# Encoder trunk: TensorE in written order, state-space work in pairs of steps, state-space input matrices made without TensorE

## The chip, the cores and the metric

One core of one Trainium2 chip runs the whole program. The metric is device time in microseconds (us) from start to end of one execution. Of the kernel before there are three runs and one profiled execution.

## The reference, cut to what matters

256 tokens of width 1024 pass through two layers, all in float32. Each layer normalises the tokens, makes one wide input projection, and feeds three branches: retention (four heads), latent attention (eight heads) and a state-space branch (S5). The branches are projected, gated and summed, projected again, and a SwiGLU feed-forward network (FFN) follows. The change lies around the S5 branch:

```python
abar_re = mag * jnp.cos(dt * a_im); abar_im = mag * jnp.sin(dt * a_im)     # 64 groups x 64 states
bb_re = coef_re[..., None] * b_re - coef_im[..., None] * b_im              # group, state, 16 channels
bu_re = jnp.einsum('bsgc,gpc->bsgp', u_g, bb_re)                           # input to the states
_, _, xr, xi = lax.associative_scan(combine, (a_re_t, a_im_t, bu_re, bu_im), reverse=reverse, axis=1)
y = jnp.einsum('bsgp,gcp->bsgc', xr, c_re) - jnp.einsum('bsgp,gcp->bsgc', xi, c_im)
```

The kernels cut the 256 tokens into 32 pieces of 8. Within a piece, the contribution of 8 tokens times 16 channels to a state is one 128 x 128 matrix per group: the input matrix, a product of powers of `abar` (8 of them) and `bb`. There are two directions and 64 groups, so a layer has 16 steps of four groups each; a step's input matrices are 128 x 1024 numbers (512 KB).

## The kernel before, in words

**Main line.** Each weight block of 512 KB (`raw`, five buffers) is fetched by SyncE (SP), which issues every DMA of the kernel. ScalarE (ACT) casts it to a high part `wh` (L668), VectorE (DVE) makes the low part `wl` (L669), and TensorE (PE) makes 24 matmuls, three per product (L673 to L675). The stages of a layer follow one another: the S5 input `u`, retention's projections and heads, the attention's projections and heads, the GLU of S5, the three branch projections, `w_out`, the FFN's gate and up, and its down projection.

**Background.** The S5 work is a Python generator, `s5` (L400). After each weight block, `tick` gives it some credit and it emits some more instructions between those of the main line. All engines are then put in an order by the framework's scheduler, TensorE too, so that what is written in one row may be taken apart.

**Input matrices.** `s5_wt` (L512) makes one step's: four DVE operations from the tables PW (powers) and BB, which lie transposed in SBUF, eight turns of 128 x 128 on PE (L536), and two ACT copies out of PSUM (L538). In layer 0 a step's matrices go at once into the products `pl` (L452: four matmuls of 32 columns by 256). In layer 1 all sixteen are made ahead, mostly under the FFN of layer 0, written to DRAM (`wtd`) and fetched again for `pl`. After two steps, `lq` is copied, turned (L462) and copied into the states SS (L467, L468).

**Output.** `s5_out` (L541) makes per step the output matrices Y (L569 to L573) and the products `pk` (L584: eight matmuls). Per pair of steps `pk` goes through DRAM (`kd`) to be skewed into M (`wt<-kd`, four loads), and `s5_emit` (L615) adds three products per step (L629: 24 matmuls per pair). The four `wt<-kd` loads take their source with an outer dimension of 8.

**Tables.** `s5_params` and `s5_tables` load a, dt and B, with B in runs of 64 bytes (`load_b`), and permute the tables with matmuls against `perm`.

Of the kernel before, what the change touches and what calls it, by code (L numbers as in the profile page):

```python
# [17 lines left out]
P = 128  # L18
# [25 lines left out]
def consts():  # L44
    c = {}
    c["ident"] = np.eye(P, dtype=np.float32)
    perm = np.zeros((P, P), np.float32)
    for d in range(2):
        for qh in range(2):
            for q in range(8):  # L50
                for g4 in range(4):
                    perm[d * 64 + (qh * 4 + g4) * 8 + q, d * 64 + (qh * 8 + q) * 4 + g4] = 1.0
    c["perm"] = perm
# [25 lines left out]
class Kern:  # L79
    def __init__(self, ctx, tc, aps, n4=17, n16=2, nraw=5, nw=3, nwl=3, nwy=3, nwt=2, ntm=2, nev=4, nat=2, r0=75, r1=75, r2=20, delay=1, late=0, e0=2, e1=0, force=0, q0=55, q1=60, nat_u=1, gauss=1, unn=1, ya=0, sp=1, yw=40, yy=30, split=2, m0=4, m1=4, fin=1, dfr=1, nu0=3, nu1=1, pin=0, nl=-1, fw=0, fy=1, ng0=0, ng1=2, tt=1, tp=0, nq0=0, nq1=0, sk=1):  # L80
# [115 lines left out]
    def exp_acc(self, out, z, n):  # L196
        nc, V = self.nc, self.nc.vector
        zc, kf, r, p = (self.s(n, f"xp{n}", 4) for _ in range(4))
        i = self.s(n, f"xi{n}", dt=I32)
# [9 lines left out]
        V.scalar_tensor_tensor(out, p, 1.0, i.bitcast(F32), ALU.add, ALU.mult)  # L209

    def s5_params(self, l):
# [19 lines left out]
        self.exp_acc(mag, z, N)  # L231
# [27 lines left out]
        cf = self.s(2 * SP_, "t_cfn").rearrange("p (r q) -> p r q", r=2)  # L259
        den, t1, t2, nr = (nt(k) for k in ("den", "t1", "t2", "nr"))  # L260
# [22 lines left out]
    def load(self):  # L283
        if self.loads:
            f = self.loads.pop(0)
            if f:
                f()

    def s5_tables(self, l):


        nc, V, A = self.nc, self.nc.vector, self.nc.scalar
        pn, cf = yield from self.s5_params(l)
        yield 4.0
        PX = self.s4().rearrange("p (j d g) -> p j d g", j=8, d=2)
        for b in range(2):
            ps = self.bank(self.p5)
            for j in range(4):
                nc.tensor.matmul(ps[:, j * P:(j + 1) * P], pn[:, b * 4 + j].rearrange("p r q -> p (r q)"),
                                 self.perm, start=True, stop=True)  # L300
            A.copy(PX[:, b * 4:b * 4 + 4].rearrange("p j d g -> p (j d g)"), ps)
        CF = self.s(2 * 64, "t_cf").rearrange("p (r g) -> p r g", r=2)
        ps = self.bank(self.p5)
        nc.tensor.matmul(ps[:, 0:P], cf.rearrange("p r q -> p (r q)"), self.perm, start=True, stop=True)
        for r in range(2):
            for d in range(2):
                A.copy(CF[d * 64:d * 64 + 64, r, :], ps[r * 64:r * 64 + 64, d * 64:d * 64 + 64])
        PW = self.s4().rearrange("p (r s g) -> p r s g", r=2, s=8)
        A8 = self.s(2 * 64, "t_a8").rearrange("p (r g) -> p r g", r=2)
        A8s = self.s(2 * 64, "t_a8s").rearrange("p (r g) -> p r g", r=2)  # L310
        for r in range(2):
            nc.gpsimd.memset(PW[0:64, r, 0, :], 1.0 - r)
            nc.gpsimd.memset(PW[64:128, r, 7, :], 1.0 - r)
            rows = slice(r * 64, r * 64 + 64)
            A.copy(PW[0:64, r, 1:8, :], PX[rows, 0:7, 0, :])
            A.copy(PW[64:128, r, 6::-1, :], PX[rows, 0:7, 1, :])
        for d in range(2):
            rows = slice(d * 64, d * 64 + 64)
            A.copy(A8[rows, 0, :], PX[0:64, 7, d, :])
            A.copy(A8[rows, 1, :], PX[0:64, 7, d, :])  # L320
            A.mul(A8s[rows, 0, :], PX[64:128, 7, d, :], -1.0)
            A.copy(A8s[rows, 1, :], PX[64:128, 7, d, :])
        PXD = self.t(self.dr, [P, 1024], "pxd", 2)
        self.dma(PXD, PX.rearrange("p j d g -> p (j d g)"))
        if l == 0 and self.nl >= 0:
            while "b" not in self.cx:
                yield None
            br, bi = self.cx.pop("b")
        else:
            br, bi = self.s4(), self.s4()  # L330
            for f in self.load_b(l, br, bi):
                f()
        BB = [self.s4(), self.s4()]
        for qh in range(2):
            c = slice(qh * 512, qh * 512 + 512)
            nat = lambda t: t[:, c].rearrange("p (h q c) -> p h q c", h=4, q=8)
            natt = lambda t: t.rearrange("p (h q c) -> p h q c", h=4, q=8)
            cfv = lambda r: (CF[:, r, qh * 32:qh * 32 + 32].rearrange("p (q h) -> p h q", h=4)
                             .unsqueeze(3).to_broadcast([P, 4, 8, GC]))
            for r, (x, y, op) in enumerate(((br, bi, ALU.subtract), (bi, br, ALU.add))):  # L340
                yield 1.9
                t1, t2 = self.s(512, "tm"), self.s(512, "tm")
                V.tensor_tensor(natt(t1), cfv(0), nat(x), ALU.mult)
                V.tensor_tensor(natt(t2), cfv(1), nat(y), ALU.mult)
                V.tensor_tensor(BB[r][:, c].rearrange("p (q h c) -> p h q c", q=8, h=4), natt(t1), natt(t2), op)
        BBD = self.t(self.dr, [P, 2048], "bbd", 2)
        for r in range(2):
            self.dma(BBD[:, r * 1024:(r + 1) * 1024], BB[r])
        PD = self.s(512, "t_pd").rearrange("p (s g) -> p s g", s=8)
        V.tensor_tensor(PD, PW[:, 1], PW[:, 0], ALU.subtract)  # L350
        V.scalar_tensor_tensor(PW[:, 1], PW[:, 1], -1.0, PW[:, 0], ALU.mult, ALU.subtract)
        BS = self.s4()
        V.tensor_tensor(BS, BB[0], BB[1], ALU.add)
        return dict(PW=[PW[:, 0], PW[:, 1], PD], PXD=PXD, A8=A8, A8s=A8s, BB=[BS, BB[1], BB[0]], BBD=BBD)

    def s5_out_tables(self, l, tb, qh):


        nc, V, A = self.nc, self.nc.vector, self.nc.scalar
        BB2 = self.s(2 * 528, "t_bb2", 1).rearrange("p (d x) -> p d x", d=2)  # L360
        for d in range(2):
            for r in range(2):
# [1137 lines left out]
```

## Time and profile before

| | |
|---|---|
| median of three runs | 1428.64 us (1426.89 to 1428.98) |
| the profiled execution | 1425.45 us, span 1423.5 us |
| mean granted TensorE clock | 0.982 |
| PE, weight loads, DVE, ACT busy | 94%, 87%, 73%, 57% of the span |
| DMA | 260.84 MB, mean 183 GB/s |
| PE chain share | 68%, then ACT 13%, DMA 8%, DVE 6% |

A busy PE is not a PE at its peak: matmuls overlap, and their ends are modelled. The engine with 94% can still be slowed by what it waits for between matmuls that the profile joins.

### The profile page before, as it was taken

Reading aid. Unit: us, or ns where it says so; the run is one execution under the profiler, and the core shown is the slowest. Engines: PE = TensorE matmul, PEld = TensorE weight load, DVE = VectorE, ACT = ScalarE, POOL = GpSimd, SP = SyncE. Lnnn points to the kernel's source line nnn. Section 1 sums busy time; section 2 is a strip of 40 time slices with the busy share of each in tenths; the row PEclk is TensorE's granted clock in tenths of the full one; section 3 lists DMA queues with packets and bytes.
Section 4 is the critical chain, followed back from the end, with each engine's and each line's share of the span. In section 5 each row is a group of like instructions: output and inputs, shape, how many; then the busy total and the mean of one; then the engine's idle time right before and its main releaser. Section 6 shows DMA issues by size and latency. Waiting matters only on the chain.

```text
span 1423.5 us, 27613 instructions
## 1 busy us (share of the span) xinstructions
PE 1334.4 (94%) x11102; PEld 1234.2 (87%) x11102; DVE 1042.3 (73%) x1910; ACT 807.0 (57%) x1339; POOL 4.5 (0%) x33
## 2 busy tenths in 40 slices
PE   7899998888999999999999999788999999999997
PEld 5866878867888999999999868778988899999997
DVE  7977867877687679988668547877768657777754
ACT  3656576974654455545446677786564344544442
POOL 0000000000000000000000000000000000000000
PEclk9999999999999999999999999999999999999999
DMA  8944233646786699766679784365687667666662
GB/s 218 250 146 118 69 104 99 182 137 152 211 219 194 201 211 260 210 199 197 188 229 273 239 267 131 99 193 156 157 247 188 193 200 204 181 185 187 179 179 79
DMA packets 433891, 260.84 MB, mean 183 GB/s; under 512 B 61714, under 2 KB 413284, under 8 KB 433764
## 3 DMA queue, kind: packets, MB, share of 16 engines
q1 hardware_dynamic: 433764, 259.09, 64.3%
q8 instruction: 87, 1.43, 0.4%
q14 instruction: 40, 0.33, 0.1%
HBM read 231.53 MB, written 27.53 MB: 182 GB/s over the span
## 4 chain that ended last, share of the span: by engine, by line
PE 68%; ACT 13%; DMA 8%; DVE 6%; issue 3%; SPq 1%; DVEq 0%; ACTq 0%
PE pw L673 17%; PE pw L674 17%; PE pw L675 17%; DMA wt<-kd 3%; ACT wh L668 3%; PE pw L713 2%; PE pw L714 2%; PE pw L715 2%; DVE wl L669 2%; DMA kd<-ev 2%; ACT s L497 2%; PE p L536 2%; PE p L452 2%; DMA raw<-in_w_in 1%; SPq L121 1%
## 5 line engine op out<-in xcount | busy, mean ns | idle before, releaser
L673 PE MATMUL pw<-s,wh 128*128 128x256 f32 x2472 | 714.6, 290 | 16.6 <-ACT wh L668 13.8
L675 PE MATMUL pw<-s,wl 128*128 128x256 f32 x2472 | 703.5, 285 | 8.4 <-DVE wl L669 8.3
L674 PE MATMUL pw<-s,wh 128*128 128x256 f32 x2472 | 703.0, 285 | 0.2 <-DVE s L749 0.2
L668 ACT CAST wh<-raw 128x1024 fp32r<-128x1024 f32 (+4 forms) x394 | 381.0, 972 | 456.2 <-PE pw L674 290.7
L669 DVE TENSOR_TENSOR wl<-raw,wh 128x1024 fp32r<-128x1024 f32 (+4 forms) x394 | 443.1, 1128 | 206.8 <-ACT wh L668 205.4
L673 PEld LDWEIGHTS pw<-s,wh 128*128 128x128 f32 x2472 | 472.1, 191 | 34.1 <-ACT wh L668 16.6
L675 PEld LDWEIGHTS pw<-s,wl 128*128 128x128 f32 x2472 | 472.5, 191 | 15.5 <-DVE wl L669 11.2
L674 PEld LDWEIGHTS pw<-s,wh 128*128 128x128 f32 x2472 | 472.9, 191 | 6.6 <-issue 4.8
L713 PE MATMUL pw<-s,wh 128*128 128x256 f32 x256 | 71.9, 281 | 0.0
L714 PE MATMUL pw<-s,wh 128*128 128x256 f32 x256 | 71.9, 281 | 0.0
L715 PE MATMUL pw<-s,wl 128*128 128x256 f32 x256 | 71.9, 281 | 0.0
L569 DVE TENSOR_TENSOR wy<-s,s 128x512 f32<-128x512 f32 x64 | 42.3, 687 | 16.1 <-PE pa L629 10.3
L715 PEld LDWEIGHTS pw<-s,wl 128*128 128x128 f32 x256 | 48.2, 188 | 0.0
L714 PEld LDWEIGHTS pw<-s,wh 128*128 128x128 f32 x256 | 48.2, 188 | 0.0
L713 PEld LDWEIGHTS pw<-s,wh 128*128 128x128 f32 x256 | 48.2, 188 | 0.0
L536 PE MATMUL p<-ident,wy 128*128 128x128 f32 x256 | 36.7, 276 | 11.5 <-ACT s L468 11.1
L497 ACT COPY s<-s 64x256 f32<-64x256 f32 (+1 forms) x64 | 40.7, 636 | 5.2 <-DVE s L483 4.3
L536 PEld LDWEIGHTS p<-ident,wy 128*128 128x128 f32 x256 | 28.6, 140 | 16.6 <-ACT s L468 13.2
L570 DVE TENSOR_TENSOR tm<-s,s 128x512 f32<-128x512 f32 x64 | 43.0, 687 | 0.0
L571 DVE TENSOR_TENSOR wy<-wy,tm 128x512 f32<-128x512 f32 x64 | 42.7, 685 | 0.0
L748 ACT ACTIVATE s<-ev 128x512 fp32r<-128x512 f32 x46 | 29.1, 633 | 19.7 <-DVE ev L1350 12.1
L531 DVE TENSOR_TENSOR wy<-wy,tm 128x1024 f32<-128x1024 f32 x32 | 39.1, 1221 | 0.3
(284 smaller groups left out, 1549.7 us busy)
## 6 DMA issues: line engine op xcount, KB each, us to landing
raw<-in_w_in SPq DMA_DIRECT2D x122, 512.0 KB
raw<-in_ffn_w_gu SPq DMA_DIRECT2D x88, 512.0 KB
raw<-in_w_branch SPq DMA_DIRECT2D x48, 512.0 KB
raw<-in_s_w_glu SPq DMA_DIRECT2D x32, 512.0 KB
raw<-in_ffn_w_down SPq DMA_DIRECT2D x32, 512.0 KB
wt<-kd SPq DMA_DIRECT2D x64, 128.0 KB
raw<-in_w_out SPq DMA_DIRECT2D x16, 512.0 KB
wtd<-wt SPq DMA_DIRECT2D x16, 512.0 KB
```

The costliest lines, as they stand in the source:

```text
L497: A.copy(*todo.pop(0))
L536: T.transpose(ps[:, i * P:(i + 1) * P], W[i % 2][:, gp * 2 + i // 2].rearrange("p s c -> p (s c)"), self.ident)
L570: V.tensor_tensor(t2, tv(1), cv(C2), ALU.mult)
L571: V.tensor_tensor(y[:, :, js, :], y[:, :, js, :], t2, ALU.add)
L668: self.nc.scalar.copy(hi, src)
L669: self.nc.vector.tensor_tensor(lo, src, hi.bitcast(F32), ALU.subtract)
L673: T.matmul(ps, lh, rh, start=first, stop=False)
L674: T.matmul(ps, lh, rl, start=False, stop=False)
L675: T.matmul(ps, ll, rh, start=False, stop=last)
L713: T.matmul(o, wh[:, k, c], xh, start=(half == 0 and m == 0 and k == 0), stop=(k == 3), **f)
L714: T.matmul(o, wh[:, k, c], xl, start=False, stop=(k == 3), **f)
L715: T.matmul(o, wl[:, k, c], xh, start=False, stop=(k == 3), **f)
```

## The change

Five things are changed. TensorE runs in the order in which the program is written (`manual_schedule`), and a `yield "later"` in the generator puts what follows behind the next weight block. The input matrices are no longer turned: the tables are written to DRAM in the layout of rows (PWD, BBD), and each step fetches them spread over the partitions (`s5_fetch`: four loads of 256 KB, 1 MB per step), whereupon four DVE operations (two of 1024 columns, two of 512) give the matrices. `pl`, `pk` and `emit` are written per pair of steps, each in one row, with `lq` turned one pair later and copied by four ACT copies of 256 columns in place of eight of 128. In the attention, the product with V of a head is written one head later, and its pools change. B, a and dt are loaded by `by_group` (16 loads of B in runs of 4 KB over the two layers); `perm` is gone, and 16 turns per layer make the table BB2D.

```diff
             return
         self.credit = min(self.credit + us * self.rate, 12.0)
         while self.credit > 0 and self.bg is not None:
-            self.step()
+            if self.step() == "later":
+                break
...
+        if c == "later":
+            return c
         self.credit -= c
...
+    def by_group(self, t, k, l, n):
+
+        v = self.a[k]
+        v = v[l:l + 1]
+        for d in range(2):
+            for qh in range(2):
+                p0 = d * 64 + qh * 32
+                self.dma(t[p0:p0 + 32], bass.AP(tensor=v.tensor, offset=v.offset + p0 * n,
+                                                ap=[[n, 8], [8 * n, 4], [1, n]]))
+
...
-    def load_b(self, l, *bs):
-
-        f = lambda t, k, d: self.dma(t[d * 64:d * 64 + 64].rearrange("p (g c) -> p g c", c=GC),
-                                     self.a[k][l, d].rearrange("g p c -> p g c"))
-        return [lambda t=t, k=k, d=d: f(t, k, d) for t, k in zip(bs, ("s5_b_re", "s5_b_im")) for d in range(2)]
...
-                continue
-            lq = self.s(512, "ev")
-            A.copy(lq, pl)
+        def turn(lq, j):
+
...
+            ptv = pt.rearrange("p (q r h n) -> p r n q h", q=2, r=2, h=4)
+            for r in range(2):
+                o = lambda rows, step: SS[rows, r, ::step, j * 8:j * 8 + 8].rearrange("p n (q h) -> p n q h", q=2)
+                A.copy(o(slice(0, 64), 1), ptv[0:64, r])
+                A.copy(o(slice(64, 128), -1), ptv[64:128, r])
+
+        lq = None
+        for j in range(8):
+            wts = []
+            for qq in (2 * j, 2 * j + 1):
+                if wtd is None:
+                    wt = yield from self.s5_wt(tb, qq)
+                    yield self.yw / 2 if self.fw else self.yw
+                else:
+                    wt = self.s(1152, "wy")[:, 0:1024]
+                    self.dma(wt, wtd[qq])
+                    yield 0.8
+                wts.append(wt.rearrange("p (d g x) -> p g d x", d=2, g=4))
+            yield "later"
+            if lq is not None:
+                turn(lq, j - 1)
+            pl = self.bank(self.p5)
+            for i, qq in enumerate((2 * j, 2 * j + 1)):
+                for g4 in range(4):
+                    T.matmul(pl[g4 * 32:g4 * 32 + 32, i * 256:i * 256 + 256],
+                             UT[qq // 8][:, qq % 8, g4 * 32:g4 * 32 + 32],
+                             wts[i][:, g4], start=True, stop=True, tile_position=(0, g4 * 32))
+            lq = self.s(1152, "wy")[:, 0:512]
+            A.copy(lq.rearrange("p (q r d x) -> p q d r x", q=2, d=2, r=2),
+                   pl.rearrange("p (q d r x) -> p q d r x", q=2, d=2, r=2))
+        yield "later"
+        yield "later"
+        turn(lq, 7)
...
+    def s5_fetch(self, tb, qq):
+
+        if qq > 15 or qq in tb["ld"]:
+            return
+        ld = tb["ld"][qq] = []
+        for k, ap in (("PWD", [[16384, 8], [0, 16], [1, 512]]), ("BBD", [[0, 8], [16384, 16], [1, 512]])):
+            t = self.s4()
+            src = tb[k][:, :]
+            for d in range(2):
+                self.dma(t[:, d * 512:(d + 1) * 512],
+                         bass.AP(tensor=src.tensor, offset=src.offset + d * 8192 + qq * 512, ap=ap))
+            ld.append(t.rearrange("p (x r q) -> p x r q", x=8, r=2))
+
     def s5_wt(self, tb, qq):
 
-        V, A, T = self.nc.vector, self.nc.scalar, self.nc.tensor
-        PW, BB = tb["PW"], tb["BB"]
-        gs = slice(qq * 4, qq * 4 + 4)
-        pwv = lambda r: PW[r][:, :, gs].rearrange("p s g -> p g s").unsqueeze(3).to_broadcast([P, 4, 8, GC])
-        bbv = lambda r: (BB[r][:, qq * 64:(qq + 1) * 64].rearrange("p (g c) -> p g c", g=4)
-                         .unsqueeze(2).to_broadcast([P, 4, 8, GC]))
...
-        wt = self.s(1024, "wt")
-        for gp in range(2):
-            ps = self.bank(self.p5)
-            for i in range(4):
-                T.transpose(ps[:, i * P:(i + 1) * P],
-                            W[i % 2][:, gp * 2 + i // 2].rearrange("p s c -> p (s c)"), self.ident)
-            A.copy(wt[:, gp * 512:(gp + 1) * 512], ps)
-        return wt
+        V = self.nc.vector
+        for q in (qq, qq + 1):
+            self.s5_fetch(tb, q)
+        pw, bb = tb["ld"].pop(qq)
+        by = lambda r: pw[:, :, r:r + 1, :].to_broadcast([P, 8, 2, SP_])
+        wt, k2 = self.s(1152, "wy"), self.s(1152, "wy")
+        k1, k2 = (t[:, 0:1024].rearrange("p (x r q) -> p x r q", x=8, r=2) for t in (wt, k2))
+        V.tensor_tensor(k1, bb, by(0), ALU.mult)
+        V.tensor_tensor(k2, bb[:, :, ::-1, :], by(1), ALU.mult)
+        if self.fw:
+            yield self.yw / 2
+        V.tensor_tensor(k1[:, :, 0, :], k1[:, :, 0, :], k2[:, :, 0, :], ALU.subtract)
+        V.tensor_tensor(k1[:, :, 1, :], k1[:, :, 1, :], k2[:, :, 1, :], ALU.add)
+        return wt[:, 0:1024]
...
@@ s5_out: the products and their outputs
-            if q % 2 == 0:
-                continue
+                Ys.append(Y)
+            yield "later"
+            if job:
+                self.s5_emit(job)
+            pk = self.bank(self.p5)
+            for i, q in enumerate(qs_):
+                for d in range(2):
+                    for g4 in range(4):
+                        gm = q * 4 + g4
+                        c0 = i * 240 + (112 if d == 0 else 0)
+                        js = slice(0, 8) if d == 0 else slice(1, 9)
+                        T.matmul(pk[g4 * 32:g4 * 32 + 32, c0:c0 + 128],
+                                 BB2[:, d, gm * 16:gm * 16 + 32],
+                                 Ys[i][d][:, g4, js, :].rearrange("p j c -> p (j c)"),
+                                 start=(d == 0), stop=True, tile_position=(0, g4 * 32), skip_group_check=(d == 1))
...
@@ after it: the job of a pair
+            job = (qs_, Ys, M, yq, UT, Sf, Sb, qh)
+        for _ in range(3):
+            yield "later"
+        self.s5_emit(job)
+        yield from self.s5_gather(job, du_load, gel_out)
...
+    def s5_emit(self, job):
...
+        qs_, Ys, M, yq, UT, Sf, Sb, qh = job
+        po = self.bank(self.p5)
+        for i, q in enumerate(qs_):
             for k in range(3):
                 for g4 in range(4):
...
-            yield 3.0
+        q0 = qs_[0]
+        A.copy(yq[:, :, q0:q0 + 2, :].rearrange("p t q c -> p q t c"),
+               po[:, 0:256].rearrange("p (q t c) -> p q t c", q=2, t=8))
+
+    def s5_gather(self, job, du_load, gel_out):
+
+        nc, V, T = self.nc, self.nc.vector, self.nc.tensor
+        yq, qh = job[3], job[7]
+        y = du_load(qh)
...
@@ attend
+        def value(hd, pts):
             if hd % 2 == 0:
-                po = self.bank(self.pa)
-            vv, hh = kvs[hd // 4][1], hd % 4
+                value.po = self.bank(self.pa)
+            po, vv, hh = value.po, kvs[hd // 4][1], hd % 4
             for kt in range(2):
                 T.matmul(po[:, (hd % 2) * S:(hd % 2 + 1) * S], vv[:, kt * 512 + hh * MV:kt * 512 + (hh + 1) * MV],
                          pts[:, kt * S:(kt + 1) * S], start=(kt == 0), stop=(kt == 1))
             if hd % 2 == 1:
                 self.put(y, hd - 1, 2, po)
+
+        pe, held = score(0), None
+        for hd in range(MH):
+            more()
+            more()
+            if held:
+                value(hd - 1, held)
+            held = turn(pe)
+            if hd + 1 < MH:
+                pe = score(hd + 1)
+        more()
+        value(MH - 1, held)
         run(work)
...
     def run(self):
+
+        with self.tc.manual_schedule(engines={mybir.EngineType.PE}):
+            self.trunk()
+
+    def trunk(self):
```

**TensorE, layer 0, the products of a step.** Before, the rows around steps 6 and 7: `p<-ident,wy` are turns of an input matrix, `p<-wt` are `pl`, `pw` is the main line (retention's value projection).

```order
L536 MATMUL p_214_1134<-ident,wy_1127 128x128 x4
L673 MATMUL pw_1152<-wh_1156,s_33_211 128x512
L674 MATMUL pw_1152<-wl_1157,s_33_211 128x512
L675 MATMUL pw_1152<-wh_1156,s_35_213 128x512
L673 MATMUL pw_1153<-wh_1156,s_33_211 128x512
L536 MATMUL p_215_1140<-ident,wy_1127 128x128 x4
L452 MATMUL p_204_1086<-wt_1133,s_124_625 32x256 x2
L674 MATMUL pw_1153<-wl_1157,s_33_211 128x512
L675 MATMUL pw_1153<-wh_1156,s_35_213 128x512
L452 MATMUL p_204_1086<-wt_1133,s_124_625 32x256 x2
L673 MATMUL pw_1152<-wh_1156,s_33_211 128x512
L674 MATMUL pw_1152<-wl_1157,s_33_211 128x512
```

And now, at the products of steps 6 and 7: `p<-ident` is the turn of `lq` of the pair before, `p<-wy` are `pl`.

```order
L695 MATMUL pw_1120<-wh_1141,s_30_225 128x512
L696 MATMUL pw_1120<-wl_1142,s_30_225 128x512
L697 MATMUL pw_1120<-wh_1141,s_32_227 128x512
L448 MATMUL p_217_1157<-ident,wy_1055 128x128 x4
L473 MATMUL p_218_1166<-wy_1063,s_134_751 32x256 x4
L473 MATMUL p_218_1166<-wy_1093,s_134_751 32x256 x4
L695 MATMUL pw_1119<-wh_1191,s_31_226 128x512
L696 MATMUL pw_1119<-wl_1192,s_31_226 128x512
```

The turns are gone, and what stood in pieces of two and four between matmuls of the main line is twelve instructions in one row, once per pair.

**SyncE, layer 0, while the products are made.** Before, the queue holds weight blocks and one table.

```order
L121 DMA raw_1302<-in_w_in 128x8x128
L121 DMA raw_1332<-in_w_in 128x8x128
L121 DMA s_243_1290<-in_rel 128x4x256
L121 DMA raw_1447<-in_w_in 128x8x128
L121 DMA raw_1477<-in_w_in 128x8x128
L121 DMA raw_1585<-in_w_in 128x8x128
L121 DMA raw_1615<-in_w_in 128x8x128
L121 DMA raw_1739<-in_w_in 128x8x128
```

Now, at the same weight blocks, the fetches (`s<-pwd`, `s<-bbd`, 256 KB each) stand between them.

```order
L114 DMA s_220_1177<-pwd_321 128x1x512 x2
L114 DMA s_221_1180<-bbd_436 128x1x512 x2
L114 DMA s_227_1207<-pwd_321 128x1x512 x2
L114 DMA s_228_1210<-bbd_436 128x1x512 x2
L114 DMA raw_1281<-in_w_in 128x8x128
L114 DMA raw_1389<-in_w_in 128x8x128
L114 DMA raw_1431<-in_w_in 128x8x128
L114 DMA s_234_1239<-in_rel 128x4x256
L114 DMA s_248_1331<-pwd_321 128x1x512 x2
L114 DMA raw_1516<-in_w_in 128x8x128
L114 DMA s_249_1334<-bbd_436 128x1x512 x2
```

Each step's fetches stand one step ahead of their use, and the weight blocks stand behind them in the queue.

**TensorE, layer 0, the output of S5.** Before, `p<-wy,t_bb` is `pk` of a step, and `pa<-wy` and `pa<-wt` are `emit` of a pair, in two places 20 rows apart.

```order
L674 MATMUL pw_3637<-wl_3659,s_418_2238 128x256
L675 MATMUL pw_3637<-wh_3658,s_418_2238 128x256
L584 MATMUL p_705_3694<-wy_3683,t_bb_621_3231 32x128 x8
L673 MATMUL pw_3710<-s_418_2238,wh_3706 128x256
```

```order
L629 MATMUL pa_3350<-wy_3498,s_443_2410 32x128 x4
L629 MATMUL pa_3350<-wy_3498,s_444_2411 32x128 x4
L629 MATMUL pa_3350<-wt_3678,s_124_625 32x128 x4
L629 MATMUL pa_3350<-wy_3575,s_443_2410 32x128 x4
L629 MATMUL pa_3350<-wy_3575,s_444_2411 32x128 x4
L629 MATMUL pa_3350<-wt_3678,s_124_625 32x128 x4
```

Now the `emit` of one pair and the `pk` of the next are one row.

```order
L697 MATMUL pw_3465<-s_235_1241,wl_3469 128x256
L646 MATMUL p_671_3496<-wy_3152,s_435_2360 32x128 x4
L646 MATMUL p_671_3496<-wy_3152,s_436_2361 32x128 x4
L646 MATMUL p_671_3496<-wt_3317,s_134_751 32x128 x4
L646 MATMUL p_671_3496<-wy_3197,s_435_2360 32x128 x4
L646 MATMUL p_671_3496<-wy_3197,s_436_2361 32x128 x4
L646 MATMUL p_671_3496<-wt_3317,s_134_751 32x128 x4
L612 MATMUL p_672_3522<-wy_3322,t_bb_601_3088 32x128 x8
L612 MATMUL p_672_3522<-wy_3363,t_bb_601_3088 32x128 x8
```

Between the `pk` of a pair and its `emit` there stand two to four weight blocks of the main line.

## Rows read from the trace of the kernel before

**Rows 1.** The page: span, the engines' busy time, and the chain's shares.

```profile
span 1423.5 us, 27613 instructions
PE 1334.4 (94%) x11102; PEld 1234.2 (87%) x11102; DVE 1042.3 (73%) x1910; ACT 807.0 (57%) x1339; POOL 4.5 (0%) x33
...
PE 68%; ACT 13%; DMA 8%; DVE 6%; issue 3%; SPq 1%; DVEq 0%; ACTq 0%
```

**Rows 2.** Windows: us from start to end, length, busy time per engine, PEclk, DMA share, GB/s.

```profile
67.40:220.60 153.20, 141.69 (x949) 111.71 (x949) 115.72 (x223) 95.51 (x174) 0.54 (x4) 0.98 0.38 111
555.70:802.20 246.50, 246.21 (x2025) 243.14 (x2024) 197.91 (x267) 126.22 (x170) 0.17 (x1) 1.00 0.75 221
1139.00:1388.00 249.00, 249.00 (x2088) 248.26 (x2087) 166.00 (x203) 117.03 (x140) 0.00 (x0) 1.00 0.64 188
```

**Rows 3.** Chain of waits, 46 to 100 us: start, us, what.

```profile
66.03 1.14 PE p L536 x8
...
69.75 0.44 PE p L536 x4
...
89.98 0.44 PE p L536 x4
```

**Rows 4.** Chain of waits, first and last products of the input matrices of layer 0.

```profile
67.41 1.07 PE p L452 x8
...
219.99 0.56 PE p L452 x4
```

**Rows 5.** What PE waits for: total us, times, longest.

```profile
PE pw L673 <- ACT wh L668: 13.8, 10, 3.9
PE pa L629 <- DMA wt<-kd: 11.3, 19, 1.1
PE p L536 <- ACT s L468: 11.1, 7, 1.8
...
PE pa L1153 <- ACT at L1146: 2.4, 2, 1.7
PE p L452 <- DMA wt<-wtd: 1.6, 2, 1.1
PE pa L1170 <- ACT at L1156: 1.4, 1, 1.4
```

**Rows 6.** Windows: `wt<-kd` alone (two rows), weight blocks, the output's store.

```profile
316.40:317.40 1.00, 1.00 (x11) 1.00 (x10) 1.00 (x2) 0.00 (x0) 0.00 (x0) 1.00 0.54 146
333.00:334.00 1.00, 0.46 (x14) 0.19 (x6) 1.00 (x2) 1.00 (x3) 0.00 (x0) 1.00 0.54 158
320.00:322.00 2.00, 1.83 (x30) 1.10 (x29) 1.44 (x4) 0.04 (x1) 0.00 (x0) 1.00 1.13 264
1419.50:1422.50 3.00, 0.00 (x0) 0.00 (x0) 0.00 (x0) 0.00 (x0) 0.00 (x0) 0.50 0.82 315
```

**Rows 7.** Groups by line: operation, busy us, mean ns, idle before.

```profile
L536 PE MATMUL p<-ident,wy 128*128 128x128 f32 x256 | 36.7, 276 | 11.5 <-ACT s L468 11.1 <-ACT wt L538 0.2
L538 ACT COPY wt<-p 128x512 f32<-128x512 f32 x64 | 35.8, 587 | 3.4 <-PE p L536 3.0
L531 DVE TENSOR_TENSOR wy<-wy,tm 128x1024 f32<-128x1024 f32 x32 | 39.1, 1221 | 0.3
L523 DVE TENSOR_TENSOR tm<-s,s 128x512 f32<-128x512 f32 x32 | 21.7, 684 | 0.1
```

**Rows 8.** Chain of waits in S5's output of layer 0.

```profile
308.51 0.36 PE p L584 x8
...
325.17 0.62 PE p L584 x16
325.81 0.57 ACT ev L598
326.40 4.36 DMA kd<-ev
...
332.65 4.84 DMA wt<-kd
337.53 1.06 PE pa L629 x26
```

**Rows 9.** Chain of waits, the wait for a weight block behind B's loads.

```profile
48.81 9.07 DMA raw<-in_w_in
```

**Rows 10.** SyncE's issues at the start: start, us, what.

```profile
0.74 0.40 SPq L121 DMA_DIRECT2D ident<-in_ident  x1
...
8.90 3.85 SPq L121 DMA_DIRECT2D raw<-in_w_in  x4
```

**Rows 11.** SyncE's issues, layer 1: first and last reloads of input matrices (16 of them).

```profile
802.48 0.57 SPq L121 DMA_DIRECT2D wt<-wtd  x1
...
862.33 2.44 SPq L121 DMA_DIRECT2D wt<-wtd  x2
```

More of the change, by code (lines that the diff above doesn't have):

```diff
@@ L323, in s5_tables @@
         PXD = self.t(self.dr, [P, 1024], "pxd", 2)
         self.dma(PXD, PX.rearrange("p j d g -> p (j d g)"))
[L325 to L339, printed above, removed]
+        BBD = self.t(self.dr, [16, 16384], "bbd", 2)
@@ L344, in s5_tables @@
[L344 to L351, printed above, removed]
@@ L352, in s5_tables @@
-        BS = self.s4()
-        V.tensor_tensor(BS, BB[0], BB[1], ALU.add)
-        return dict(PW=[PW[:, 0], PW[:, 1], PD], PXD=PXD, A8=A8, A8s=A8s, BB=[BS, BB[1], BB[0]], BBD=BBD)
+                t1, t2 = (self.s(512, "tm").rearrange("p (c q) -> p c q", c=8) for _ in range(2))
+                V.tensor_tensor(t1, cfv(0), nat(x, hf), ALU.mult)
+                V.tensor_tensor(t2, cfv(1), nat(y, hf), ALU.mult)
+                V.tensor_tensor(B[:, :, r, :], t1, t2, op)
+            rows(BBD, hf * 8, B.rearrange("p c r q -> p c (r q)"))
@@ new lines, in s5_tables @@
+            BB.append(B)
+        del br, bi
+        BB2D = self.t(self.dr, [P, 2048], "bb2d", 2)
+        half = [self.s4().rearrange("p (d x c) -> p d x c", d=2, x=32) for _ in range(2)]
+        yield "later"
+        for c4 in range(4):
+            ps = self.bank(self.p5)
+            for i in range(4):
+                c = c4 * 4 + i
+                T.transpose(ps[:, i * P:(i + 1) * P], BB[c // 8][:, c % 8].rearrange("p r q -> p (r q)"), self.ident)
+            v = ps.rearrange("p (c d k x) -> p c d k x", c=4, d=2, k=2)
+            for qh in range(2):
+                A.copy(half[qh][:, :, :, c4 * 4:c4 * 4 + 4].rearrange("p d x c -> p c d x"), v[:, :, :, qh])
+            if c4 % 2:
+                yield "later"
@@ L421, in s5 @@
             uq = u[qh].rearrange("p (x s) -> p x s", s=8)
+            yield "later"
             for sb in range(2):
@@ new lines, in s5_out @@
+            yield "later"
+            if job:
+                self.s5_emit(job)
+            pk = self.bank(self.p5)
+            for i, q in enumerate(qs_):
+                for d in range(2):
+                    for g4 in range(4):
[6 more added lines that the diff above has]
+                                 start=(d == 0), stop=True, tile_position=(0, g4 * 32), skip_group_check=(d == 1))
@@ new lines, in s5_emit @@
+        A.copy(yq[:, :, q0:q0 + 2, :].rearrange("p t q c -> p q t c"),
[4 more added lines that the diff above has]
+        y = du_load(qh)
+        yield "later"
+        dv = yv = y.rearrange("p (x s) -> p s x", s=8)
+        for sb in range(2):
+            ps = self.bank(self.p5)
+            for i in range(4):
+                T.transpose(ps[:, i * P:(i + 1) * P],
+                            yq[:, sb * 4 + i].rearrange("p q c -> p (q c)"), self.ident)
+            V.tensor_tensor(yv[:, sb * 4:sb * 4 + 4, :], ps.rearrange("p (s x) -> p s x", s=4),
+                            dv[:, sb * 4:sb * 4 + 4, :], ALU.add)
+        gel_out(qh, y)
+        yield 3.0
@@ L1119, in more @@
             done[0] += 1
-            while done[1] < done[0] * steps // 16:
+            while done[1] < done[0] * steps // 17:
                 done[1] += 1
@@ L1239, in layer @@
             dus.append(du)
-            if not (l == 0 and self.nl >= 0):
-                self.dma(dud[:, qh * 1024:(qh + 1) * 1024], du)
-        while self.loads:
-            self.load()
-        if l == 0 and self.nl >= 0:
-            for qh in range(2):
-                self.dma(dud[:, qh * 1024:(qh + 1) * 1024], dus[qh])
+            self.dma(dud[:, qh * 1024:(qh + 1) * 1024], du)
         del du, dus
```

267 lines of the change are left out of this document (90 added, 177 removed).

## Prediction, made before the changed kernel ran

> **What bounds the kernel now.** I read the page first. PE is busy for 94% of the span and holds 68% of the chain of waits; ACT comes next with 13% [rows 1]. So the time follows what TensorE has to do plus what it waits for, and busy time alone does not tell the two apart. The windows do [rows 2]. From 1139 to 1388 us, the FFN of layer 1, PE is busy throughout, DMA's share is 0.64 and nothing else is in the way. From 67.4 to 220.6 us, where the input matrices of layer 0 are made and used, PE is busy for 141.7 of 153.2 us and the share of DMA is only 0.38. From 555.7 to 802.2 us, where the matrices of layer 1 are made beside the FFN of layer 0, PE is full (246.2 of 246.5 us) and DMA's share is 0.75. Third, the list of what PE waits for: 13.8 us for the high parts of weights, 11.3 us for the skewed matrices of S5's output, 11.1 us in which the turns of input matrices wait for ACT [rows 5].
>
> **A. Layer 0, making and using input matrices (153.2 us).** Sixteen steps follow from 67.41 to 219.99 us [rows 4], one each 9.6 us. Four turns take 0.44 us on the chain [rows 3], so 128 turns are 14.1 us; the waits of turns for ACT, 11.1 us [rows 5], lie in this stretch and go with them; and `pl`, eight matmuls of which cost 1.07 us together and four 0.56 us [rows 4], gain little from pairing beyond the way in and out, say 5 us for 16 pieces that become 8. By TensorE alone the stretch falls by 30 to 123 us. DVE, 115.7 us busy [rows 2], gets two operations of 1024 columns (1.22 us) and two of 512 (0.68) for one of 1024 and three of 512 [rows 7]: 3.8 for 3.3 us a step, 8 us in all, which its 37 free us hold. ACT loses two copies of 587 ns a step [rows 7].
>
> What is late next is DMA. Each step now fetches 1.05 MB. The trace has one kind of load whose source has an outer dimension of 8 as these fetches have, `wt<-kd`: while it runs alone, DMA's share is 0.54 and 146 to 158 GB/s move; weight blocks have a share of 1.13 at 264 GB/s [rows 6]. So such a load keeps half of the engines busy. What it moves on its half depends on the length of a run: `kd` has 512 bytes, the fetches 2 KB as the store of the output has, which moves 315 GB/s at a share of 0.82, 384 at full, 192 on half [rows 6]. The bounds of a fetch are 5.5 us (192 GB/s) and 6.9 us (151 GB/s); the run length speaks for 5.5. On those engines the stretch holds 0.38 x 153.2 = 58 us of other transfers and 14 fetches (two are ahead of it), 77 us: 135 us. At 6.9 us it would be 155. TensorE's 123 us do not decide then. I take 135: **-18 us** (-30 to +2).
>
> The Trainium skill, DMA: Bandwidth & Descriptors, "Why a DMA increments its semaphore by 16 and not by 1", says that a copy is split over the largest number of engines, at most 16, that divides the slowest dimension of both of its patterns; by it a source of 8 x 16 rows goes to 8 engines, which is against this change, and the trace's 0.54 agrees.
>
> **B. Layer 1's input matrices (246.5 us).** The same 128 turns go: -14 us for TensorE, which would be 232. DMA's share of 0.75 [rows 2] is 185 us of each engine; 14 of the 16 fetches in the stretch add 77 us to the half that serves them: 262 us (282 at 6.9 us). Five raw buffers cannot bridge this, since the fetches stand ahead of weight blocks in SyncE's queue, as the order shows for layer 0. So here the change costs: **+16 us** (-14 to +35). Where fetches spread into the start of layer 1 it is less.
>
> **C. Pieces that become rows, outside A and B.** By the code, S5's products interrupt the main line in the two layers with 32 `pk`, 16 `emit` and, in layer 1, 16 `pl`; afterwards with 18 rows of `emit` and `pk` and 8 `pl`: 38 fewer. Eight `pk` take 0.36 us and sixteen 0.62 [rows 8], so an interruption saved is worth 0.1 us at least; two `pl` groups show 0.56 for four against 1.07 for eight, nothing at all [rows 4]. A leaving of the small tiles that delays the next matmul as a turn does (0.44 us for four) is the upper bound: 38 x 0.1 to 0.6 is 4 to 23. I take 0.26: **-10 us**.
>
> **D. Start.** The wait of 9.07 us for a weight block that landed behind B's loads in 64-byte runs [rows 9] goes, since B now comes in runs of 4 KB. Against it 16 more issues stand ahead of the first weight block, at 0.40 us and a gap, 7 us [rows 10]: **-2 us** (-9 to +7).
>
> **E. Layer 1, reloading input matrices.** Before, 16 reloads are issued between 802.48 and 862.33 us, one each 4 us [rows 11], and PE waits only 1.6 us for them [rows 5]. Now both of a pair share four buffers with `lq` and are asked for a pair ahead at most; a pair takes one weight block, 2.83 us (249 us for 88), plus its turn and products, 1.5 us. Two reloads of 524 KB at 264 GB/s are 4.0 us plus the way. Losing the eight small copies of states per pair against four (ACT) is for it. I take **-5** (-12 to +10).
>
> **F. The wait of `emit`.** From the end of `pk` the path is 0.57 + 4.36 + 1.9 (issues) + 4.84 us, 11.7 us in all [rows 8]. In the new order two to four weight blocks stand between, 5.7 to 11.3 us, with matmuls of attention on top (about 2 us). The scheduler could put `emit` later where it was late; the written order cannot. Sixteen pairs short by 1 us on average are 17 against 11.3 now [rows 5]: **+6** (-11 to +30).
>
> **G. Ends of stages.** The scheduler filled them with the next block's matmuls; the written order does not. One such wait (L673 for a wait on ACT) is within the 13.8 us of [rows 5], so a place costs 1 to 3 us; few are bare: **+2** (0 to +25).
>
> **H. ACT and the attention.** ACT loses 64 copies of 587 ns (35.8 us) [rows 7] and half of the state copies. What PE waits for high parts is 13.8 us, for attention's weights 2.4 and 1.4 [rows 5], and the product with V now comes a head later: of 17.6 us I take two thirds, **-12** (-18 to 0).
>
> **Sum.** -18 + 16 - 10 - 2 - 5 + 6 + 2 - 12 = -23 us on the profiled 1425.45 us: 1402. The median of the three runs is 3.2 us above the profiled execution, so 1406 for a median.
>
> **Rivals.** *The fetches reach all engines.* Then A and B are TensorE's: -30 and -14 for -18 and +16, 42 us less: 1364. For it speaks that the fetches repeat rows within a step (16 readers of a row), which `kd` does not; against it 0.54 in [rows 6].
>
> *The half-width fetches bound both stretches.* One mechanism, in A and B, at 6.9 us a fetch: A +2, B +35, with C to H (-21) +16, and fetches that queue ahead of weight blocks make it no better: 1445. The other terms are -21, and A and B together are 28 fetches plus 243 us against 399.7, so from 6.35 us a fetch (165 GB/s) the change is slower. For it: 146 to 158 GB/s in [rows 6]. Against it: the runs are four times as long.
>
> *The written order gives it back.* A to E and H as forecast, but G is at its 25 and F stays: 1402 + 23 + 3 = 1428, no change. For it: the scheduler's order leaves PE only some 89 us idle (1423.5 less 1334.4 [rows 1]). Against it: most of PE's waits [rows 5] are of one place each.
>
> **How the numbers follow.** Chances: forecast 0.42, all engines 0.20, half-width bound 0.24, written order 0.14. Within 0.2%, about 2.9 us, is no change. Faster: 0.41 of the forecast's, 0.20, 0.02 and 0.04 of the others, 0.67; no change 0.08; slower 0.25. The range goes from the first rival to the second, 1360 to 1445; the forecast's own is 1390 to 1422.
>
> **What would show it.** A is right if the products of layer 0 lie between 130 and 140 us apart from first to last, with DMA's share near 0.8 in that window and DVE's input-matrix operations waiting for fetches; a share near 0.54 while only fetches run shows the half. B is right if the FFN of layer 0 takes longer than that of layer 1 per weight block, with waits of `wh` for `raw`. D is wrong if the first native matmul is not about 7 us later. F shows as `emit` waiting for `wt<-kd` for more than 11 us. The forecast is wrong altogether if a fetch's megabyte lands in 3 us, or if PE's waits at the ends of stages sum to over 20 us.

## The result: slower by 9%

The changed kernel takes 1557.17 us (median of 4 runs, 1554.35 to 1557.51) against 1428.81 us of the kernel before beside it (4 runs, 1426.89 to 1431.27): a ratio of 1.089, with a 95% interval of 1.087 to 1.091. The prediction was 1406 us, and the range ended at 1445. The direction was wrong, too.

The page of the changed kernel: the span is 132 us longer, PE's busy time is the same, and ACT has lost 49 us ([rows 1] before).

```profile
span 1555.7 us, 27234 instructions
PE 1331.0 (86%) x10858; PEld 1254.1 (81%) x10858; DVE 1066.0 (69%) x1904; ACT 757.7 (49%) x1223; POOL 4.4 (0%) x33
```

The mean granted clock fell from 0.982 to 0.935. Windows of the changed kernel, columns as in [rows 2]: the products of layer 0's input matrices, the FFN of layer 0 with layer 1's matrices, and the FFN of layer 1.

```profile
80.00:268.00 188.00, 137.74 (x928) 118.91 (x927) 135.12 (x250) 75.25 (x129) 0.65 (x4) 0.85 0.62 180
580.00:846.00 266.00, 231.06 (x1750) 225.43 (x1749) 183.07 (x255) 100.80 (x131) 0.00 (x0) 0.93 0.83 225
1380.00:1530.00 150.00, 150.00 (x1267) 150.00 (x1267) 99.21 (x118) 68.00 (x79) 0.00 (x0) 1.00 0.64 182
```

Stages with fetches lose: in the first PE is busy for 73% of the time at a granted clock of 0.85, in the second for 87% at 0.93. The FFN of layer 1, where nothing is fetched, is as full as it was. Other stages without fetches lose as well; a table further down counts them. What PE waited for on the low parts of weights before, which [rows 5] leaves out, and what it waits for now (columns as in [rows 5]):

```profile
PE pw L675 <- DVE wl L669: 8.3, 10, 3.1
```

```profile
PE pw L697 <- DVE wl L691: 43.1, 22, 5.1
PE pw L695 <- ACT wh L690: 29.9, 9, 6.1
PE pa L834 <- ACT ev L827: 15.3, 5, 6.2
PE p L473 <- DVE wy L552: 15.2, 2, 10.3
PE pw L747 <- DMA raw<-in_w_in: 14.5, 1, 14.5
PE pa L988 <- ACT at L981: 14.4, 2, 7.4
PE p L473 <- DMA wy<-wtd: 10.9, 6, 3.6
PE p L646 <- DMA wt<-kd: 8.1, 13, 1.1
```

The waits for high and low weight parts went from 13.8 and 8.3 us to 29.9 and 43.1 us. New are the ends of norms and heads (L834, L988), the wait of the products for VectorE (L473) and the first native matmul (L747). The wait for the skewed matrices (L646) fell from 11.3 to 8.1 us. VectorE's group that multiplies what was fetched (line, busy us, mean ns | idle before):

```profile
L547 DVE TENSOR_TENSOR wy<-s,s 128x1024 f32<-128x1024 f32 x32 | 39.1, 1222 | 68.3 <-DMA s<-bbd 55.6 <-DMA raw<-in_w_in 7.9 <-issue 2.6
```

It waits 55.6 us for `bbd` fetches, and all weight parts `wl` behind it in VectorE's queue wait with it. At the start SyncE issues 20 loads of the S5 parameters ahead of the weight blocks, one each 0.71 to 0.76 us. Before, the parameters there were three loads, of which a load of `a_re` took 0.43 us, and the first weight block was issued at 8.90 us ([rows 10]) in place of 21.01. The row of before, then those of the changed kernel:

```profile
7.48 0.43 SPq L121 DMA_DIRECT2D s<-in_s_a_re  x1
```
```profile
3.53 3.04 SPq L114 DMA_DIRECT2D nt_ldt<-in_s_log_dt  x4
...
9.45 2.88 SPq L114 DMA_DIRECT2D s<-in_s_b_re  x4
12.37 2.84 SPq L114 DMA_DIRECT2D s<-in_s_b_im  x4
15.25 2.84 SPq L114 DMA_DIRECT2D s<-in_s_a_re  x4
18.13 2.84 SPq L114 DMA_DIRECT2D s<-in_s_a_im  x4
21.01 4.10 SPq L114 DMA_DIRECT2D raw<-in_w_in  x4
```

### The profile page after: what moved, and what is told of

It is laid out like the page before. It is cut to its first block, busy times and chain, and to the rows that moved or that the text cites. A ratio compares the mean times of both kernels' runs of the same rounds, so it can differ in the third digit from the quotient of the medians.

```text
span 1555.7 us, 27234 instructions
## 1 busy us (share of the span) xinstructions
PE 1331.0 (86%) x10858; PEld 1254.1 (81%) x10858; DVE 1066.0 (69%) x1904; ACT 757.7 (49%) x1223; POOL 4.4 (0%) x33
## 5 line engine op out<-in xcount | busy, mean ns | idle before, releaser
L695 PE MATMUL pw<-s,wh 128*128 128x256 f32 x2440 | 720.9, 295 | 37.3 <-ACT wh L690 29.9
L697 PE MATMUL pw<-s,wl 128*128 128x256 f32 x2440 | 708.5, 290 | 43.2 <-DVE wl L691 43.1
L696 PE MATMUL pw<-s,wh 128*128 128x256 f32 x2440 | 707.1, 290 | 6.4 <-DVE s L770 4.1
L695 PEld LDWEIGHTS pw<-s,wh 128*128 128x128 f32 x2440 | 482.7, 198 | 49.9 <-ACT wh L690 32.2
L697 PEld LDWEIGHTS pw<-s,wl 128*128 128x128 f32 x2440 | 482.1, 198 | 49.0 <-DVE wl L691 48.8
L696 PEld LDWEIGHTS pw<-s,wh 128*128 128x128 f32 x2440 | 482.7, 198 | 10.9 <-DVE s L770 5.3
L547 DVE TENSOR_TENSOR wy<-s,s 128x1024 f32<-128x1024 f32 x32 | 39.1, 1222 | 68.3 <-DMA s<-bbd 55.6
L735 PE MATMUL pw<-s,wh 128*128 128x256 f32 x256 | 75.5, 295 | 6.2 <-ACT s L766 6.0
L736 PE MATMUL pw<-s,wh 128*128 128x256 f32 x256 | 75.0, 293 | 1.8 <-DVE s L767 1.8
L735 PEld LDWEIGHTS pw<-s,wh 128*128 128x128 f32 x256 | 51.2, 200 | 7.4 <-ACT s L766 6.5
L736 PEld LDWEIGHTS pw<-s,wh 128*128 128x128 f32 x256 | 51.3, 201 | 2.3 <-DVE s L767 2.3
L737 PEld LDWEIGHTS pw<-s,wl 128*128 128x128 f32 x256 | 51.2, 200 | 1.0 <-DVE wl L691 1.0
L473 PE MATMUL p<-wy,s 128*32 128x256 f32 x256 | 21.2, 438 | 26.2 <-DVE wy L552 15.2
L595 DVE TENSOR_TENSOR tm<-s,s 128x512 f32<-128x512 f32 x64 | 43.1, 685 | 0.2
L747 PE MATMUL pw<-s,raw 128*128 128x256 f32 x128 | 30.2, 395 | 14.5 <-DMA raw<-in_w_in 14.5
```

The costliest lines, as they stand in the source:

```text
L595: V.tensor_tensor(t2, tv(1), cv(C2), ALU.mult)
L695: T.matmul(ps, lh, rh, start=first, stop=False)
L696: T.matmul(ps, lh, rl, start=False, stop=False)
L697: T.matmul(ps, ll, rh, start=False, stop=last)
L735: T.matmul(o, wh[:, k, c], xh, start=(half == 0 and m == 0 and k == 0), stop=(k == 3), **f)
L736: T.matmul(o, wh[:, k, c], xl, start=False, stop=(k == 3), **f)
```

## The experiments

Each was timed in rounds beside the kernel before (1428 to 1431 us), and a difference between two of them is one of medians. Five theories were at work: fetches on half of the engines; the written order of TensorE; the fetches as such; the pairs; the attention's order.

**e1, full-width fetches.**

```diff
-("PWD", [[16384, 8], [0, 16], [1, 512]]), ("BBD", [[0, 8], [16384, 16], [1, 512]])
+("PWD", [[0, 16], [16384, 8], [1, 512]]), ("BBD", [[16384, 16], [0, 8], [1, 512]])
```

(u and M follow the same order of rows.)

> The rows of the input matrices are put in the order channel, piece position (16 x 8) in place of 8 x 16, so that every fetch of the tables has an outer dimension of 16; the same bytes, the same runs of 2 KB, the same number of loads. The skewed matrices of S5's output are loaded in eight loads with an outer dimension of 16 in place of four with 8. Theory 1 (fetches on half of the engines hold back VectorE's queue, and the half clock that follows the waits adds to it): VectorE's waits for fetches (36 us in the FFN of layer 0, 8 us in layer 0's products) fall to under 10 us, the FFN of layer 0 loses some 30 us, layer 0's products some 15: 1480 to 1510 us. Theory 2 (TensorE's written order is the loss, whatever the fetches do): 1535 to 1560 us.

Measured 1528.75 us (1.067, 1.064 to 1.071): 28 us, about 60% of the least that theory 1 asked, and more than theory 2 allowed. VectorE's wait for `bbd` fell from 55.6 to 32.9 us in all, not to under 10; against the gain, TensorE's wait for the skewed matrices, now in eight loads, rose from 8.1 to 15.2 us. Windows in which little but fetches moves, of the changed kernel and of e1:

```profile
100.00:112.00 12.00, 10.40 (x52) 8.73 (x53) 8.88 (x12) 3.85 (x5) 0.00 (x0) 0.71 0.53 203
```
```profile
100.00:108.00 8.00, 8.00 (x40) 6.87 (x41) 6.43 (x7) 2.22 (x4) 0.00 (x0) 0.61 1.06 290
```

At these rates, a step's fetch of 1.05 MB takes 5.2 us at half width (share 0.53, 203 GB/s) and 3.6 us at full (1.06, 290 GB/s).

**e2, the scheduler's order for TensorE.**

```diff
-        with self.tc.manual_schedule(engines={mybir.EngineType.PE}):
-            self.trunk()
+        self.trunk()
```

> The changed kernel with TensorE ordered by the scheduler again, as all other engines are; nothing else is touched. Theory 1 (half-width fetches): the stretches with fetches stay slow, since VectorE's order does not change; 1520 to 1560 us. Theory 2 (the written order): 1430 to 1470 us, with the ends of stages and the waits of S5's output filled again.

Measured 1509.14 us (1.054, 1.050 to 1.057): 48 us, more than theory 1 allowed and less than theory 2 asked. Each is a part. VectorE waits even longer for `bbd` in this run, 71.1 us for 55.6.

**e5, both.**

> Fetches with an outer dimension of 16 and TensorE ordered by the scheduler. If the two causes add: the gains of the two runs alone summed, 1557 less both. If they are one chain (the written order only passes on the late fetches): no more than the better of the two alone.

Measured 1460.78 us (1.022, 1.017 to 1.026): 96 us less, where 28 and 48 would sum to 76. They more than add, so neither of the two expectations holds: full width is worth 48 us once the order is the scheduler's.

**e3, weight blocks ahead of the parameters.**

```diff
+        self.first = [self.wraw(... OFF_U + m * P ...) for m in range(4)]
         self.begin(0)
```

> The first four weight blocks are issued ahead of the 24 loads of the S5 parameters. Both theories: the first native matmul starts near 9 us in place of 25, and the first cast of a weight block 10 to 14 us earlier. If the start is 13 us of the loss by itself: 1541 to 1547 us. If the tables, which then come 2 us later, set the start of layer 0's products anyway: 1553 to 1558 us.

Measured 1548.17 us (1543.81 to 1557.69), 9 us less by the median and between the two ranges. The profiled execution is the slowest of the four, 1557.69 us, and shows no gain, so where the median's 9 us come from is not shown. PE of e3 (start, us, line, operation, wait before it):

```profile
30.22 0.35 PE L855 MATMUL p<-ident,at 66*128 66x66 f32 x1 [18.49 <-DMA at<-in_final_g]
30.36 6.25 PE L747 MATMUL pw<-s,raw 128*128 128x256 f32 x16
```

The native matmuls (those that take a weight block as it is, without high and low parts) begin at 30.36 us, later than the 25.28 us without the edit: in the written order a turn of the norms' vectors stands ahead of them, and its load now came last. The weight blocks were moved ahead of the 20 loads, and the row found another reason to wait.

**e6, turns in place of fetches**, with scheduler, pairs and the attention's order (`s5_params`, `s5_tables`, `s5_wt` and `s5_out_tables` of before in the changed kernel).

> The changed kernel with the input matrices made by turns as before (no fetches; the tables and their loads as before, too), and with TensorE ordered by the scheduler; the pairs of steps and the attention's order are those of the change, with one of 17 buffers fewer. If the fetches are what is left of the loss in the run with full-width fetches and the scheduler (1461 us): 1415 to 1435 us, at or under the kernel before. If pairs and the attention's order cost too: 1440 to 1465 us.

Measured 1430.61 us (0.999, 0.997 to 1.002): no change. So fetches at full width, with their tables and loads, cost 30 us more than the 256 turns and 64 copies that they replace (e5 less e6), and what is left of the change nets nothing. Not all of the 30 is the fetches': the run takes back the loads of the parameters, too, and its first cast of a weight block starts 15 us earlier than that of e5 (e5, then e6):

```profile
45.24 1.04 ACT L692 CAST wh<-raw 128x1024 fp32r<-128x1024 f32 x1 [1.26 <-DMA raw<-in_w_in]
```
```profile
30.20 1.04 ACT L698 CAST wh<-raw 128x1024 fp32r<-128x1024 f32 x1 [2.34 <-DMA raw<-in_w_in]
```

**e14, half of the fetched bytes**, on e5 (the powers are fetched once a layer, which halves the loads as well as the bytes; one of 17 buffers fewer).

```diff
+            if k == "PWD" and "pwk" in tb:
+                ld.append(tb["pwk"])
+                continue
```

> Full-width fetches and the scheduler (1461 us), where each layer fetches the powers of the first step only, so that a step fetches 512 KB in place of 1 MB (all later steps multiply with the first step's powers; that part of the computation is left out). If what the fetches cost at full width is the time of DMA (its share is 0.95 in the FFN of layer 0 there): the share falls by 0.1 or more, VectorE's waits for fetches from 34 us to under 12, and the time to 1432 to 1447 us. If it is the place of the fetches, one step ahead of VectorE whatever their size: 1453 to 1463 us.

Measured 1438.34 us (1.005, 1.002 to 1.008): 22 of the 30 us. Windows over the FFN of layer 0, with turns (e6), with all fetches at full width (e5) and with half of the bytes (e14):

```profile
530.00:757.00 227.00, 222.45 (x1822) 219.46 (x1821) 187.15 (x272) 109.87 (x148) 0.00 (x0) 0.99 0.74 213
```
```profile
545.00:785.00 240.00, 224.19 (x1774) 219.13 (x1773) 182.81 (x255) 102.43 (x132) 0.00 (x0) 0.97 0.95 254
```
```profile
540.00:775.00 235.00, 229.53 (x1877) 226.61 (x1876) 191.91 (x265) 109.37 (x142) 0.00 (x0) 0.99 0.87 242
```

DMA's share is 0.74, 0.95 and 0.87; VectorE's wait for `bbd` fell from 34.2 to 12.1 us. The share fell by 0.08 where 0.1 was expected, and the wait came out a little above 12; the time lies in the range that was named for DMA's time. From its first cast to the first cast behind it, the FFN of layer 0 takes 201 us in e6, 213 in e5 and 197 in e14, so there half of the fetches cost nothing. What the fetches cost at full width is thus their amount; bytes and number of loads were not told apart. The late start stays: the first cast is at 46.5 us in e14.

**e9, fetches two steps ahead**, on e5 (`for q in (qq, qq + 1, qq + 2)`).

> Full-width fetches and the scheduler (1461 us) with the fetches asked for two steps ahead in place of one. VectorE waits 34 us for fetches there. If the distance of one step is what makes it wait: the waits fall by half or more and the time by 8 to 20 us, to 1441 to 1453 us. If the buffers are given back too late for it: 1455 to 1465 us.

Measured 1462.91 us: nothing gained; VectorE's wait fell only from 34.2 to 26.4 us. Distance alone is no help here; whether a full DMA or buffers that come back late hold the fetches, this run does not tell.

**e10, the attention's order of before**, on e5.

> Full-width fetches and the scheduler (1461 us) with the attention's product with V back in the place that it had before. From the 54th to the 90th weight block that run loses 24 us against the kernel before. If the attention's order is the cause: 1440 to 1450 us. If it is the pairs of S5's output: 1457 to 1465 us.

Measured 1458.19 us (1453.97 to 1462.8): 3 us, within what the runs tell apart; by this run the attention's order is not the cause of the 24 us.

**e8, the skew at full width in the kernel before.**

> The kernel before with one edit: the order channel, piece position in its input matrices, so that the skewed matrices of S5's output come in eight loads with an outer dimension of 16 in place of four with 8. TensorE waits 11.3 us for them before. If the half-width load is that wait: 1420 to 1426 us. If the four more issues of 0.6 us eat it: 1428 to 1434 us.

Measured 1436.12 us (1.0035, 1.0015 to 1.0056), above both ranges. The wait for `wt<-kd` did fall, from 11.3 to 6.4 us, but the new order of rows makes VectorE write with strides, and three operations a step went from 684 ns ([rows 7]) to 1166 to 1184. One of the three in e8:

```profile
L524 DVE TENSOR_TENSOR tm<-s,s 128x512 f32<-128x512 f32 x32 | 37.1, 1171 | 0.1
```

The three are 47 us more of VectorE's time over the run; how much of the loss is theirs and how much the four more issues' was not tried.

**e11, the products in pairs alone**, in the kernel before: eight `pl` in a row, the turn of `lq` one pair later, four copies.

```diff
-            for g4 in range(4):
-                T.matmul(plv[g4 * 32:g4 * 32 + 32, :], ...)
+            if lq is not None:
+                turn(lq, j - 1)
+            for i, qq in enumerate((2 * j, 2 * j + 1)):
+                for g4 in range(4):
+                    T.matmul(pl[..., i * 256:i * 256 + 256], ...)
```

> The kernel before with one part of the change: the products of the input matrices in pairs of steps, eight matmuls in a row, the turn of lq one pair later, its states copied by four ACT copies of 256 columns in place of eight of 128 (one more wy buffer, one s4 buffer fewer). The scheduler orders TensorE; turns and S5's output are those of before. In the run with turns, pairs and scheduler (1431 us) the 42nd weight block comes 31 us earlier than before, and 24 of it are given back by the 90th. If the pairs of products are the gain and the pairs of S5's output the loss: 1400 to 1415 us. If the gain is given back by whatever follows: 1425 to 1433 us.

Measured **1400.91 us** (0.979, 0.974 to 0.983): faster than both kernels. The stretch of A in e11, from its first to its last products (76.8 to 196.1 us by PE's records):

```profile
76.50:196.00 119.50, 118.84 (x919) 105.30 (x918) 107.43 (x214) 78.55 (x133) 0.55 (x4) 1.00 0.46 125
```

It takes 119 us where the kernel before takes 153, and PE is busy for 99% of it. Since it begins 9 us later than before, the kernel is 27 us ahead behind it, and 22 at the end. Of the 34 us, 11 are idle time of PE, 11.5 before ([rows 2]) and 0.7 here; in the rest PE counts as busy. By the starts of PE's records, the `pl` matmuls took 147 ns each before, to the next start, and 63 ns here: 18.5 and 8.0 us in all. Whether the row of eight, the later turn or the fewer copies does it was not tried apart.

**e12, S5's output as before**, on e6.

> The run with turns, pairs and scheduler (1431 us) with S5's output (pk, emit and the last turns) as before, step by step; the attention's order stays that of the change. If the pairs of S5's output give the 24 us back: 1405 to 1418 us. If the attention's order does: 1427 to 1435 us.

Measured 1419.43 us (0.993, 0.991 to 0.996), between the two ranges. So output in pairs costs 11 us (e6 less e12), and what separates e12 from e11 (the attention's order and its pools, the later places that `yield "later"` gives, two scratch buffers in place of four in the scan over the states) costs 18.5 us. That was not split further; e10 speaks for little from the attention alone.

**e13, a head's last step one place later**, on e1.

> Full-width fetches in written order (1529 us) with the last step of a retention head, whose turns wait 14.1 us in two places for ACT, written behind the next head's value and score matmuls. If the loss of the written order is that such places are waited for where they are written: these waits fall under 5 us and the time by 6 to 20 us (the waits and the half clock behind them). If the wait moves to the next instruction of the row: 1524 to 1532 us.

Measured 1525.88 us, 3 us less than e1. The wait only moved:

```profile
PE pa L968 <- DVE at L961: 19.2, 4, 9.4
PE pa L836 <- ACT ev L829: 15.3, 5, 6.2
```

L968, the head's value products, now waits 19.2 us for VectorE; the turns that waited 14.1 us in e1 no longer do. L836, the end of a norm, waits as it did.

## Why the prediction was wrong, point by point

One path from before to after, by medians: `pl` in pairs -28 (e11); the attention's order, later places and pools +19 (e12); output in pairs +11 (e6); fetches at full width, with their tables and loads, for turns +30 (e5), of which some 15 are the start; half width +48 (e2); written order +48 (after). The sum, +128, is the result's, as a path's must be; another path gives other shares (half width is 28 in written order).

By stages: ACT casts 394 weight blocks to high parts (`wh<-raw`) in every run, so the n-th cast marks the same place of the main line. The table has what a profiled execution loses against that of the kernel before from one such cast to another, in us, rounded; a minus is a gain.

| stage, by casts | forecast | changed | e2 | e5 | e11 |
|---|---|---|---|---|---|
| start, to the 1st | D -2 | +13 | +18 | +17 | +1 |
| layer 0's products, to the 39th | A -18 | +17 | -7 | -32 | -28 |
| rest of layer 0, to the 128th | C, F, G, H | +17 | +30 | +27 | +3 |
| FFN of layer 0, to the 196th | B +16 | +44 | +33 | +14 | 0 |
| layer 1's products, to the 234th | E -5 | +15 | +3 | -4 | -1 |
| rest of layer 1, to the 327th | C, F, G, H | +25 | +9 | +15 | +3 |
| FFN of layer 1, to the end | none | +3 | 0 | 0 | 0 |
| all | -23 | +132 | +85 | +36 | -22 |

In e2 and e5 the last products come some 20 us behind the 39th cast, so part of their price stands in the next row. Every term that the forecast gave to a stage came out worse, and the rest of the two layers, where C, F, G and H were in the main to gain 14 us together, lost 42.

- **A (-18) and B (+16), failed in the way they were summed.** The price of a fetch was right: 5.5 us forecast, 5.2 measured, on half of the engines as [rows 6] showed. The step that failed is "TensorE's 123 us do not decide then. I take 135", with 262 us for B: the slower of two totals was taken for the time of a stretch. Layer 0's products take 161 us from first to last (95.6 to 256.2 by PE's records) at a DMA share of 0.63, where 135 at a share near 0.8 was forecast, and they begin 28 us later than before. The FFN of layer 0 takes 243 us by its casts, for 199 before. No engine's total is the time there; the wait of one step passes down a chain. In the FFN of layer 0 VectorE waits for fetches (36.0 of its 55.6 us lie between 606 and 808 us), the weight parts behind in its queue are late, and PE waits for them, 17.5 us for low parts in the same window. In layer 0's products VectorE's wait for fetches is only 8.0 us; PE waits there 15.2 us for the first matrices (L473) and 14.4 us for the ends of heads (L988). The rival that had both stretches bound by DMA was priced by the same totals at 1445 and was therefore too low, too. So was the rival in which the fetches reach all engines: e1 and e5 are that case, at 1529 and 1461 us for 1364.
- **G (+2) and F (+6), the written order, mis-sized.** F came out at 8.1 us for 11.3, better than forecast. The rest of the order was put at 2 us "few are bare", bound 25, and is worth 48 to 68 us (after less e2; e1 less e5). The forecast's own sign, waits at the ends of stages of over 20 us, did show: L834 and L988 alone are 29.7 us. It is not only the ends of stages: whatever comes late from VectorE or ACT stops the row where it stands, as e13 and e3 show. The rival "the written order gives it back" had this mechanism, and its bound was too small.
- **The clock, left out.** The granted clock falls behind waits. From 1242 to 1247 us PE waits four times for `wt<-kd`, up to 1.1 us, and the matmuls behind it take 0.41 us in place of 0.28 until 1250.4 us; then it waits 3.9 and 0.9 us for the parts of an activation (high on ACT, L766; low on VectorE, L767), and the matmuls take 0.41 us again until 1263.9. Windows ahead of the first wait and behind the second:

```profile
1230.00:1241.50 11.50, 11.50 (x157) 11.17 (x157) 5.01 (x6) 4.58 (x6) 0.00 (x0) 1.00 0.77 241
1256.00:1264.00 8.00, 6.17 (x28) 5.97 (x29) 1.23 (x1) 1.59 (x2) 0.00 (x0) 0.58 0.62 197
```

The grant is 1.00 ahead (2.4 GHz) and 0.58 behind, mostly the lower level of 1.2 GHz. The mean loss of grant is 0.065 of 1555.7 us against 0.018 of 1423.5: 101 against 26 us of full-speed time, a bound of 75 us on what waits cost beyond themselves, since some of it falls into idle time.
- **C (-10), wrong, with a gain at another place.** Outside A and B, where C was forecast, the output in pairs cost 11 us (e12, e6), and the pairs of layer 1's products gained about 1 (e11). In stretch A the pairs gained 28 us, where A put the 8 interruptions saved at 5 us. The gain of A that the forecast gave to the end of the turns was to be had with the turns in place.
- **D (-2):** the first native matmul came 10 us later (25.28 for 15.28), not 7, since each of the 20 loads took 0.71 us and not 0.43. And the 9.07 us that were to go were a step of the chain, not a stop of PE, which stood idle for 3.3 us of them in the kernel before:

```profile
48.80:58.00 9.20, 5.90 (x46) 5.29 (x45) 9.20 (x14) 5.24 (x9) 0.00 (x0) 1.00 1.13 305
```

- **E (-5):** PE waits 10.9 us for the reloads, against 1.6: the other end of its range. With the scheduler's order it is 0.7 us (e2).
- **H (-12), wrong:** ACT did give up 49 us, and PE's waits for `wh` doubled all the same. In e6, where ACT keeps the 64 copies, they are 14.4 us. ACT's load was not what they were about.

## What to carry to other kernels

A stretch in which two engines have about 90% of the work of a third (TensorE's 123 and VectorE's 124 of 135 us here) need not be bounded by the fullest: add up the chain that one step passes through, in the order of its queues. Before a strict order is put on the busiest engine, ask for every operand what is late by how much; here the scheduler's order filled gaps worth 48 to 68 us. Try the parts of a change alone: one of them, the products in pairs, was worth 28 us, and all the others together lost 156.

## What the runs showed of the hardware that was not expected

Loads whose source's outer dimension is 8 move 203 GB/s at a share of 0.53, and 290 GB/s at 1.06 with an outer dimension of 16, with runs of 2 KB in both. The parameters' loads of 32 partitions take 0.68 us to issue (one each 0.71 us), where a load of `a_re` took 0.43 before. Their outer dimension of 8 does not explain it: the issue of a fetch has a median of 0.58 to 0.61 us with 8 (changed kernel) and of 0.59 with 16 (e1). A DVE multiplication of 512 columns that writes with a stride of 8 elements took 1171 ns for 684 (e8). Behind four waits of at most 1.1 us the granted clock fell to 0.50 for some 3 us (changed kernel, 1247 to 1250.4 us).
